# A planned hybrid trunk kernel on one core: paired coupling products, PSUM banks and weight buffers freed later, y split when landed, a masked quarter filled first

## The chip, the cores and the metric

The kernel runs on one core of a Trainium2 chip. The metric is the device time of one execution in microseconds (us). Three runs of the kernel before gave 2273.69, 2272.05 and 2272.64 us; their median is 2272.64.

## The reference

One layer over 2048 positions of width 1024, all in f32. An RMS norm is followed by one input projection, whose columns feed two groups of heads.

```python
proj = einsum('bsd,de->bse', rmsnorm(h, norm_w), w_in)
# group A, 8 groups of 128 columns, blocks of 128 positions
y_a = gelu(u) * (W_masked @ layernorm(gelu(v)) + b) * silu(z)     # W: 128x128, the block (first 64, last 64) is masked
# group B, 8 heads of 128, chunks of 64 positions
q, k, v = silu(causal_conv(qkv));  q, k = l2norm(q) / sqrt(128), l2norm(k)
A = strict_lower((k * beta) @ k.T * L);  T = inverse(A + I)
u = T @ (v * beta);  w = T @ (k * beta * exp(decay));  qk = q @ k.T * L
for each chunk:  v_new = u - w @ S;  o = q_dec @ S + qk @ v_new;  S = S * a + k_dec.T @ v_new
y_b = rmsnorm(o) * norm_w * silu(z)
h = h + concat(y_a, y_b) @ w_out
h = h + sigmoid(rmsnorm(h) @ w_gate) * rmsnorm(p @ w_ple);  out = rmsnorm(h)
```

The state S runs through all chunks of a head in order, and T is the inverse of a unit lower triangular matrix.

## The kernel before

The 2048 positions are worked in two passes of 1024, each of two blocks b of 512. A pass has four units for v of group A (v_unit, lines 498 to 534) and then, for each of eight heads h, three units of 256 columns of w_in: kq_unit (lines 677 to 692), vu_unit (636) and zz_unit (648). A unit projects its 256 columns as four PSUM banks of 128 columns by 512 positions (proj, line 398). Every f32 factor of a large product is split into a high and a low part of type f32r (split, line 211), and each product is made of three matmuls: high by high, high by low, low by high (mm3, line 215). So a bank takes 8 x 3 = 24 matmuls of 512 columns. After the second pass come the output projection (out_stream, 1111), with y read back from DRAM, and the gate (gate_stream, 1254).

Beside the projection, TensorE (PE) has small work for the heads. In front (line 730) k is transposed into the bank pk, from which ACT sums squares and DVE makes kd; the products pkq of two chunks at a time give AT and QK. Two chunks of 64 are handled as one pair of 128. AT goes to DRAM, and inverse (line 838) lays all systems of a head across 128 partitions and solves them by 63 steps on POOL, reading ain in 16 pieces. The two inverses of a pair come back into the diagonal quarters of AT. join (line 887) then couples the two halves of each pair with four products pgt. chain (line 901) runs the state through the eight pairs of a head, and finish (line 974) normalises, transposes into po_t and stores y.

The order of all instructions is written out by a planner that runs when the kernel is built (Flow, lines 31 to 100). It keeps a clock for PE (fl.t) and one for DVE, ACT and POOL, adds a modelled cost for each instruction, and runs its tasks as Python generators: a task yields the time at which it wants to go on, and among those that are due the one with the lowest priority number goes first. The stream of projections is issued between the tasks. On the chip every engine runs its instructions in the order in which they were issued, and semaphores hold them back where data is not ready. All loads and stores go through the queue of SyncE (SP).

Buffers and banks are counted: take (line 68) waits until a place is free, give (line 73) returns it. CAPS (line 105) holds the counts: two PSUM banks each for pj, tr and m, four raw tiles for loaded weights, five split weight pairs w. A give stands right behind the instruction that reads the bank last, so that the place counts as free when that reader is issued. later (line 288) gives a place back at a stated time:

```python
        def later(tag, at):
            yield at
            fl.give(tag)
```

load_w (line 247) loads the four quarters of a unit's weights into raw; split_w (line 256) makes hi on ACT and lo on DVE. The first quarter of the next unit is split in the middle of a unit, the others at k = 1, 3 and 5 of its last bank (rest_w, line 281), when the running unit gives its own pairs back. y_feed (line 1063) loads pieces of y into the raw tiles and splits each as soon as a w place is free; it is started ahead of the last zz_unit, behind refill (line 1026), which loads and splits w_out. zz_unit loads ws, then clears its masked quarter (lines 650 to 652). v_unit keeps ab and the head's first state S0 in tiles of their own.

Of the kernel before, what the change touches and what calls it, by code (L numbers as in the profile page):

```python
# [103 lines left out]
SPARE = 120.0  # L104
CAPS = {"pj": 2, "tr": 2, "m": 2, "kq": 5, "pre": 2, "acc": 3, "uz": 3, "ot": 2, "gn": 2, "R": 2, "raw": 4, "w": 5}
TABLES = {AF.Exp: 1, AF.Sigmoid: 2, AF.Silu: 3, AF.Gelu_apprx_tanh: 4}


def trunk(tc, a, out):
# [78 lines left out]
    with ExitStack() as outer:  # L188
# [58 lines left out]
        def load_w(i):  # L247
            if i < len(units):
                while i and (i - 1, 3) not in W:
                    yield fl.t + 200  # L250
                for kp in range(4):
                    yield from fl.take("raw")
                    raws[i, kp] = wp.tile([P, 2, 256], F32, tag="raw", bufs=4, name="raw")
                    dma(raws[i, kp], a["wu"][units[i], kp])
# [143 lines left out]
        def proj(X, ui, c, b, mid=None):  # L398
            yield pj_free
            fl.used["pj"] = fl.used.get("pj", 0) + 1  # L400
            ps = bank("pj", "pj", [P, 512])
            cc = slice(c * P, c * P + P)
            for k in range(NK):
                if c == 0 and b == 0 and k % 2 == 0:
                    yield lambda: (ui, k // 2) in W
                hi, lo = W[ui, k // 2]
                yield from mm3(ps, hi[:, k % 2, cc], lo[:, k % 2, cc], X[k][0][:, b], X[k][1][:, b],
                               k == 0, k == NK - 1)
                if b and c and k % 2:
                    fl.give("w")  # L410
                if mid and k in mid:
                    mid[k]()
            return ps

        def proj_both(X, ui, c, mid):

            banks = []
            for b in range(2):
                yield pj_free
                fl.used["pj"] = fl.used.get("pj", 0) + 1  # L420
                banks.append(bank("pj", "pj", [P, 512]))
            cc = slice(c * P, c * P + P)
            for k in range(NK):
                hi, lo = W[ui, k // 2]
                for b in range(2):
                    yield from mm3(banks[b], hi[:, k % 2, cc], lo[:, k % 2, cc], X[k][0][:, b], X[k][1][:, b],
                                   k == 0, k == NK - 1)
                if k % 2:
                    fl.give("w")
                mid[k]()  # L430
            return banks
# [66 lines left out]
        def v_unit(X, p, ui, n, stats):  # L498

            fetch(ui + 1)  # L500
            rest = rest_w(ui + 1)
            ab = gt("ab", "ab", [P, 16, 8], 1) if n == 0 else None
            w = 256 if n else 272
# [6 lines left out]
            for group, where in groups:  # L510
# [6 lines left out]
                for k in range(NK):  # L517
                    if p == 0 and n == 0:
                        yield lambda: xready[group[0] // 4] > k
                    yield lambda: len(X) > k and (ui, k // 2) in W  # L520
                    hi, lo = W[ui, k // 2]
                    for t, tag, ps in banks:
                        tk = slice((t % 4) * P, (t % 4) * P + P)
                        yield from mm3(ps[:, :w], X[k][0][:, t // 4, tk], X[k][1][:, t // 4, tk],
                                       hi[:, k % 2, :w], lo[:, k % 2, :w], k == 0, k == NK - 1)
                    if group[-1] == 7:
                        if k % 2:
                            fl.give("w")
                        if k in rest:
                            rest[k]()  # L530
# [15 lines left out]
        def mix(p, g, gz, ws, bs, gns, norms):  # L546
# [10 lines left out]
            for b in range(2):  # L557
# [12 lines left out]
                f = stt(gn, pm, lng[:, g:g + 1], bs[:, None, :].to_broadcast([P, 4, P]), ALU.mult, ALU.add)  # L570
                fl.give("m")
                yf = gn.rearrange("p a b -> p (a b)")
# [75 lines left out]
        def zz_unit(X, p, ui, h, st, norms, mids):  # L648
            fetch(ui + 1)
            ws = gt("ws", "ws", [P, P], 1)  # L650
            dma(ws, a["ws"][h])
            nc.vector.memset(ws[64:128, 0:64], 0.0)
            bs = gt("bs", "bs", [P, P], 1)
            dma(bs, bsd[h] if p else a["bs"][h])
# [46 lines left out]
        def decay(p, h, b, i):  # L701
# [22 lines left out]
            f = act(L, pd, AF.Exp, after=f)  # L724
            fl.give("m")
            yield f + LAZY
# [3 lines left out]
        def front(p, h, b, st):  # L730
# [33 lines left out]
            for u2 in range(2):  # L764
                while len(st["C"][b]) < 2:
# [17 lines left out]
                for j in range(2):  # L783
# [9 lines left out]
                fl.give("m")  # L793
            nc.vector.memset(AT[0:64, :, 64:128], 0.0)
# [8 lines left out]
            fl.spawn(side(b, st, kq, vn, iv, ss, qe), 0, 2)  # L803
            st["B"].append((kq, kd, vn, AT, QK, bn, fb, qe, nb))
            if b == 1:
# [6 lines left out]
        def side(b, st, kq, vn, iv, ss, qe):  # L812
# [5 lines left out]
            f = yield from squares(pq, ss, 4, f)  # L818
            fl.give("tr")
            yield f  # L820
# [11 lines left out]
            yield from fl.room("dve")  # L832
            tt(vn, pv, iv[:, :, None].to_broadcast([P, 4, P]), ALU.mult)
            fl.give("tr")
            fl.give("acc")
            st["R"].append(b)

        def inverse(p, h, st):
# [37 lines left out]
            for b in range(2):  # L876
                for d in range(2):
                    dd = slice(d * 64, d * 64 + 64)
                    dma(st["B"][b][3][dd, :, dd], td[:, b, :, d])
            st["S"] = gt("S0", "S0", [P, P], 1) if p else None  # L880
            if p:
                dma(st["S"], ssc[h])
            fl.spawn(join(0, st), 6500, 0)
            fl.spawn(join(1, st), 7100, 1)
            fl.spawn(chain(p, h, st), 6500, 0)

        def join(b, st):

            M, fb = st["B"][b][3], st["B"][b][6]
            yield from fl.take("tr")  # L890
            pg = bank("tr", "pgt", [P, 4, 64])
            for u in range(4):
                f = mm(pg[:, u], M[:, u], M[:, u, 64:128], True, True)
            yield f
            f = tt(M[0:64, :, 64:128], pg[0:64], fb[0:64, :, None].to_broadcast([64, 4, 64]), ALU.mult)
            fl.give("tr")
            nc.vector.memset(M[64:128, :, 0:64], 0.0)
            yield fl.op("dve", 250) + SPARE
            st["G"].append(b)

        def chain(p, h, st):
# [6 lines left out]
            for b in range(2):  # L908
                kq, kd, vn, M, QK, bn, fb, qe, nb = st["B"][b]
                yield from fl.take("ot")  # L910
# [63 lines left out]
        def finish(p, h, b, st, ot, sso, qe, f):  # L974
# [14 lines left out]
            f = stt(y, pt.rearrange("p a b -> p (a b)"), gdnw, y, ALU.mult, ALU.mult)  # L989
            fl.give("tr")  # L990
            yield f + 200
# [71 lines left out]
        def y_feed():  # L1063
            tiles = {}

            def load(i):
                _, t, e4 = order[i]
                tk = slice((t % 4) * P, (t % 4) * P + P)
                tiles[i] = wp.tile([P, 4, P], F32, tag="raw", bufs=4, name="yraw")
# [26 lines left out]
        def out_piece(WO, key, ps, free):  # L1096
# [3 lines left out]
            for e in range(4):  # L1100
# [6 lines left out]
                if e % 2:  # L1107
                    free.append(1)
            fl.give("w")

# [143 lines left out]
        def gate_stream():  # L1254
            for t in range(NT):
# [14 lines left out]
                for half in range(2):  # L1270
# [3 lines left out]
                    for k in range(NK):  # L1274
# [6 lines left out]
                        if half and k % 4 == 3:  # L1281
                            fl.give("w")
                    if half == 1:
# [3 lines left out]
        def stream():  # L1287
            X = X0
            ui = 0
            for p in range(NPASS):  # L1290
                stats = gt("stats", "stats", [P, 8, 4, 6], 1)
                for n in range(4):
# [137 lines left out]
```

## Time and profile before

| what | value |
|---|---|
| median of three runs | 2272.64 us |
| the profiled execution's own time | 2273.43 us |
| its span, first to last instruction | 2271.7 us |
| mean granted TensorE clock | 0.995 |
| busy: PE / DVE / ACT / POOL | 98% / 59% / 47% / 49% of the span |
| largest share of the chain that ended last | PE 87% |
| DMA | 254.59 MB, 112 GB/s over the span |

The profile shows one execution. "Busy" is the time in which an engine runs at least one instruction. A matmul is recorded from its start to its end, and matmuls overlap, so the distance from one start to the next tells what a matmul costs; the recorded length is longer. A f32 matmul is recorded as two. In a timeline, like instructions that follow one another are merged and counted (x8); the bracket behind a row gives the engine's idle time before it and what ended it.

### The profile page before, as it was taken

How to read it: one execution, taken by the hardware profiler on the slowest of the kernel's cores; microseconds unless marked ns; L12 is line 12 of the kernel's file. 1: busy time of each engine (PE TensorE's matmuls, PEld its weight loads, DVE VectorE, ACT ScalarE, POOL GpSimd, SP SyncE). 2: the span in 40 equal slices, each digit the busy share in tenths (PEclk: the TensorE clock that was granted, in tenths of full speed). 3: DMA queues.
4: the chain of work that ended last, by engine and by line, in shares of the span. 5: the costliest groups of instructions: out<-in, count | busy, mean ns of one | idle time of the engine just before them, and what ended most of it. 6: DMA issues, size and time to landing. Idle time of an engine off the chain costs nothing.

```text
span 2271.7 us, 35525 instructions
## 1 busy us (share of the span) xinstructions
PE 2228.3 (98%) x11888; PEld 1888.4 (83%) x11888; DVE 1335.0 (59%) x2947; ACT 1078.3 (47%) x2541; POOL 1120.3 (49%) x2246
## 2 busy tenths in 40 slices
PE   8999999999999999999999999999899999999998
PEld 8988888888888889988888888888788878878886
DVE  4475675675676664456667567567564243356665
ACT  5554464554554644445546555455433232244443
POOL 1018868687686682058866868768550000001111
PEclk9999999999999999999999999999999999999999
DMA  5733323323323253232332332332453475452221
GB/s 168 250 100 106 101 74 97 97 81 108 95 77 105 72 174 93 81 106 77 94 100 77 94 92 80 108 97 77 137 181 122 145 232 171 141 169 84 84 75 58
DMA packets 269432, 254.59 MB, mean 112 GB/s; under 512 B 67905, under 2 KB 200513, under 8 KB 269249
## 3 DMA queue, kind: packets, MB, share of 16 engines
q1 hardware_dynamic: 269248, 252.32, 36.2%
q8 instruction: 94, 1.54, 0.3%
q14 instruction: 90, 0.73, 0.1%
HBM read 196.68 MB, written 55.57 MB: 111 GB/s over the span
## 4 chain that ended last, share of the span: by engine, by line
PE 87%; DVE 3%; ACT 3%; DMA 3%; POOL 1%; issue 1%; SPq 1%; DVEq 0%; POOLq 0%; ACTq 0%
PE pj L123 41%; PE pso L123 15%; PE pg L123 8%; PE pv L123 7%; PE pc L123 5%; PE po L123 2%; PE pkq L123 2%; PE pe L123 2%; ACT junk L137 1%; PE pm L123 1%; PE pgt L123 1%; PE po_t L129 1%; DMA ws<-in_ws 1%; PE ph L129 1%; PE pq L129 1%
## 5 line engine op out<-in xcount | busy, mean ns | idle before, releaser
L181 POOL TENSOR_TENSOR xtmp<-ain,xs 128x132 f32<-128x132 f32 (+47 forms) x1008 | 460.3, 457 | 269.5 <-DMA ain<-atd 198.7
L181 POOL TENSOR_TENSOR xs<-xs,xtmp 128x132 f32<-128x132 f32 (+47 forms) x1008 | 475.7, 472 | 79.0
L177 POOL TENSOR_TENSOR rstd<-rstd,nhalf 128x1 f32<-128x1 f32 x64 | 45.9, 723 | 576.6 <-DVE rstd L161 295.6
L123 PE MATMUL pj<-xrhi,whi 128*128 128x512 f32 x768 | 312.2, 407 | 0.0
L123 PE MATMUL pj<-xhi,wlo 128*128 128x512 f32 x768 | 310.2, 404 | 0.0
L123 PE MATMUL pj<-xrhi,wlo 128*128 128x512 f32 x768 | 309.9, 404 | 0.0
L123 PE MATMUL pj<-xrlo,whi 128*128 128x512 f32 x768 | 309.9, 403 | 0.0
L123 PE MATMUL pj<-xhi,whi 128*128 128x512 f32 x768 | 309.4, 403 | 0.0
L123 PE MATMUL pj<-xlo,whi 128*128 128x512 f32 x768 | 308.6, 402 | 0.0
L154 DVE SCALAR_TENSOR_TENSOR acc<-pre,cw,acc 128x512 f32<-128x512 f32 x288 | 224.5, 779 | 37.6 <-ACT acc L137 32.9
L150 DVE TENSOR_TENSOR wlo<-raw,whi 128x512 fp32r<-128x512 f32 x224 | 165.7, 742 | 119.0 <-ACT whi L137 116.7
L123 PE MATMUL pso<-wolo,yhi 128*128 128x512 f32 x512 | 204.0, 399 | 0.6 <-DVE wolo L150 0.5
L123 PE MATMUL pso<-wohi,ylo 128*128 128x512 f32 x512 | 203.8, 398 | 0.0
L123 PE MATMUL pso<-wohi,yhi 128*128 128x512 f32 x512 | 202.9, 396 | 0.4 <-ACT zb L137 0.4
L137 ACT ACTIVATE yhi<-yraw 128x512 fp32r<-128x512 f32 x128 | 80.3, 630 | 217.5 <-PE pso L123 203.1
L150 DVE TENSOR_TENSOR ylo<-yraw,yhi 128x512 fp32r<-128x512 f32 x128 | 89.8, 703 | 148.9 <-ACT yhi L137 142.0
L137 ACT ACTIVATE whi<-raw 128x512 fp32r<-128x512 f32 x224 | 139.1, 625 | 62.4 <-PE pj L123 25.8
L123 PEld LDWEIGHTS pj<-xrhi,wlo 128*128 128x128 f32 x768 | 145.4, 189 | 26.2
L123 PEld LDWEIGHTS pj<-xlo,whi 128*128 128x128 f32 x768 | 144.8, 189 | 26.3
L123 PEld LDWEIGHTS pj<-xrhi,whi 128*128 128x128 f32 x768 | 145.5, 189 | 25.4 <-ACT z L137 0.2
L123 PEld LDWEIGHTS pj<-xhi,whi 128*128 128x128 f32 x768 | 145.0, 189 | 25.4
L123 PEld LDWEIGHTS pj<-xrlo,whi 128*128 128x128 f32 x768 | 145.4, 189 | 24.8
(196 smaller groups left out, 4923.8 us busy)
## 6 DMA issues: line engine op xcount, KB each, us to landing
raw<-in_wu SPq DMA_DIRECT2D x224, 256.0 KB
ain<-atd SPq DMA_DIRECT2D x256, 128.0 KB
yraw<-ysc SPq DMA_DIRECT2D x128, 256.0 KB
vsc<-gv SPq DMA_DIRECT2D x64, 128.0 KB
gn<-vsc SPq DMA_DIRECT2D x32, 256.0 KB
ysc<-gn SPq DMA_DIRECT2D x32, 256.0 KB
ysc<-zb SPq DMA_DIRECT2D x32, 256.0 KB
wo<-in_wo SPq DMA_DIRECT2D x32, 256.0 KB
```

The source lines that it names most:

```text
L123: nc.tensor.matmul(o, lhsT, rhs, start=start, stop=stop)
L129: nc.tensor.transpose(o, i, ident)
L137: nc.scalar.activation(o, i, func, **kw)
L150: nc.vector.tensor_tensor(o, x, y, op)
L154: nc.vector.scalar_tensor_tensor(o, x, sc, y, op0, op1)
L177: nc.gpsimd.tensor_tensor(o, x, y, ALU.pow)
L181: nc.gpsimd.tensor_tensor(o, x, y, op)
```

## The change

It has eight parts.

1. The coupling in join: front now writes the scaled quarter to a tile of its own, XC, for all 128 partitions (ex[:, 3] in place of ex[64:128, 3]), and join makes two products for two pairs each, 128 x 128, in place of four with 64 columns. Of each result two quarters are used, one from partitions 0 to 63, one from 64 to 127. fb is copied to the partitions 64 to 127 for this, and the memset of AT's lower left quarter in join goes.
2. The banks of tr and m that were given back when their last reader was issued are given back when the planner expects that reader to have ended, plus 100 ns.
3. The w places are given back 500 ns later.
4. There are three raw tiles and not four.
5. y_feed waits until 5500 ns behind the issue of a piece's load before it takes a w place and splits.
6. In zz_unit the masked quarter of ws is cleared first, and the load comes in two parts that leave it out.
7. The first state of a head in the second pass is loaded by a task of its own, state_in, into the rotating tiles S, once the previous head's chain is planned; chain waits for it.
8. ab and stats live in the tiles of XC.

```diff
-CAPS = {..., "raw": 4, "w": 5}
+CAPS = {..., "raw": 3, "w": 5}
...
                 if b and c and k % 2:
-                    fl.give("w")
+                    fl.spawn(later("w", fl.t + 500))
...
-            ab = gt("ab", "ab", [P, 16, 8], 1) if n == 0 else None
+            ab = gt("XC", "ab", [P, 16, 8], 4) if n == 0 else None
...
             ws = gt("ws", "ws", [P, P], 1)
-            dma(ws, a["ws"][h])
             nc.vector.memset(ws[64:128, 0:64], 0.0)
+            fl.op("dve", 120)
+            dma(ws[0:64], a["ws"][h, 0:64])
+            dma(ws[64:128, 64:128], a["ws"][h, 64:128, 64:128])
...
-            tt(kd, pk, ex[:, 1, cs, None].to_broadcast([P, 4, P]), ALU.mult, after=f)
-            fl.give("tr")
+            fk = tt(kd, pk, ex[:, 1, cs, None].to_broadcast([P, 4, P]), ALU.mult, after=f)
+            fl.spawn(later("tr", max(f1, fk) + 100))
...
             tt(fb, bn, ex[:, 3, cs], ALU.mult)
+            vcopy(fb[64:128], fb[0:64])
...
+            XC = gt("XC", "XC", [P, 4, 64], 4)
...
-                tt(AT[64:128, us, 0:64], pkq[64:128, :, 0, 0:64],
-                   ex[64:128, 3, c:c + 2, None].to_broadcast([64, 2, 64]), ALU.mult)
+                tt(XC[:, us], pkq[:, :, 0, 0:64], ex[:, 3, c:c + 2, None].to_broadcast([P, 2, 64]), ALU.mult)
...
-                fl.give("m")
+                fl.spawn(later("m", f + 100))
...
-            st["S"] = gt("S0", "S0", [P, P], 1) if p else None
-            if p:
-                dma(st["S"], ssc[h])
+            fl.spawn(state_in(p, h, st), 0, 0)
...
+        def state_in(p, h, st):
+            while len(chained) < st["i"]:
+                yield fl.t + 300
+            if p:
+                st["S"] = gt("S", "S0", [P, P], 2)
+                dma(st["S"], ssc[h])
+            else:
+                st["S"] = None
...
-            pg = bank("tr", "pgt", [P, 4, 64])
-            for u in range(4):
-                f = mm(pg[:, u], M[:, u], M[:, u, 64:128], True, True)
-            yield f
-            f = tt(M[0:64, :, 64:128], pg[0:64], fb[0:64, :, None].to_broadcast([64, 4, 64]), ALU.mult)
+            pg = bank("tr", "pgt", [P, 2, 2, 64])
+            for i in range(2):
+                f = mm(pg[:, i], XC[:, 2 * i:2 * i + 2].rearrange("p u j -> p (u j)"),
+                       M[:, 2 * i:2 * i + 2, 64:128], True, True)
+            yield f
+            for j in range(2):
+                half = slice(j * 64, j * 64 + 64)
+                f = tt(M[0:64, j:4:2, 64:128], pg[half, :, j], fb[half, j:4:2, None].to_broadcast([64, 2, 64]),
+                       ALU.mult)
             fl.give("tr")
-            nc.vector.memset(M[64:128, :, 0:64], 0.0)
-            yield fl.op("dve", 250) + SPARE
+            yield f + SPARE
...
-            while len(chained) < st["i"] or len(st["R"]) < 2:
+            while len(chained) < st["i"] or len(st["R"]) < 2 or "S" not in st:
...
             def load(i):
+                at[i] = fl.t + 5500
...
+                yield at[i]
                 yield from fl.take("w")
```

The same later gives stand in proj_both, v_unit, out_piece and gate_stream (w), in mix and decay (m), and in side and finish (tr).

## Rows read from the trace of the kernel before

**Rows 1.** The page's first part: busy us, share of the span, instructions.
```profile
PE 2228.3 (98%) x11888; PEld 1888.4 (83%) x11888; DVE 1335.0 (59%) x2947; ACT 1078.3 (47%) x2541; POOL 1120.3 (49%) x2246
```

**Rows 2.** PE's waits: what waited for what, us in total, times, longest.
```profile
PE po_t L129 <- DVE kd L150: 7.2, 5, 1.6
PE pc L123 <- ACT r L137: 6.8, 2, 6.4
...
PE pkq L123 <- DVE kqlo L150: 2.8, 9, 0.5
...
PE pc L123 <- DVE w L159: 1.8, 3, 1.1
...
PE pc L123 <- DVE r L154: 0.9, 2, 0.7
```

**Rows 3.** Timeline of PE at a mix and at a join: start, us, what.
```profile
193.70 1.05 PE L123 MATMUL pm<-ws,gn 128*128 128x128 f32 x8
194.51 0.47 PE L123 MATMUL pj<-xhi,wlo 128*128 128x512 f32 x1
...
1606.18 1.00 PE L123 MATMUL pgt<-AT 128*128 128x64 f32 x8
1607.02 0.44 PE L123 MATMUL pc<-S,kq 128*128 128x128 f32 x2
```

**Rows 4.** Groups of PE instructions: count, busy us, mean ns, idle before.
```profile
L123 PE MATMUL pgt<-AT 128*128 128x64 f32 x256 | 31.5, 270 | 0.5 <-DVE AT L150 0.5
```

**Rows 5.** Groups of DVE instructions around the join.
```profile
L150 DVE TENSOR_TENSOR AT<-pkq,ex 64x128 f32<-64x128 f32 x64 | 18.8, 294 | 2.2
L150 DVE TENSOR_TENSOR AT<-pgt,fb 64x256 f32<-64x256 f32 x32 | 13.3, 414 | 15.0 <-PE pgt L123 14.7
...
L897 DVE MEMSET AT<- 64x256 f32 x32 | 8.7, 272 | 3.0
```

**Rows 6.** Timeline from 503 us: DVE's kd and PE's transposes.
```profile
503.17 0.69 DVE L150 TENSOR_TENSOR kd<-pk,ex 128x512 f32<-128x512 f32 x1 [0.63 <-ACT junk L137]
...
503.91 0.66 PE L129 MATMUL po_t<-ident,ot 128*128 128x128 f32 x4 [1.42 <-DVE kd L150]
```

**Rows 7.** Timeline from 1609 us: the first y loads, their split, PE.
```profile
1609.29 2.81 SPq L1070 DMA_DIRECT2D yraw<-ysc  x4
...
1615.32 0.63 ACT L137 ACTIVATE yhi<-yraw 128x512 fp32r<-128x512 f32 x1 [9.69 <-DMA yraw<-ysc]
...
1616.64 0.80 PE L123 MATMUL pc<-r,AT 128*128 128x128 f32 x2 [6.44 <-ACT r L137]
```

**Rows 8.** Stretches: us; busy (count) of PE, PEld, DVE, ACT, POOL; PEclk; DMA.
```profile
125.00:827.00 702.00, 693.28 (x3642) 581.78 (x3641) 463.30 (x1073) 370.11 (x916) 501.69 (x1015) 1.00 0.33 98
...
1600.00:1605.00 5.00, 5.00 (x25) 4.11 (x24) 1.47 (x4) 4.25 (x12) 0.00 (x0) 1.00 0.54 136
...
1617.00:1622.00 5.00, 5.00 (x16) 4.13 (x16) 0.99 (x3) 0.79 (x4) 2.65 (x8) 0.50 0.81 222
```

**Rows 9.** Tile pc from 505 to 575 us: ns min/median/max, first and last start.
```profile
L123 PE MATMUL pc<-w,kd x16: 270/274/323, 527.3 to 572.6; 128*128 128x128 f32 x16
```

**Rows 10.** DVE's waits: us in total, times, longest.
```profile
DVE ws L652 <- DMA ws<-in_ws: 33.7, 14, 6.3
```

**Rows 11.** Timeline from 1341 us: the memset of ws and PE behind it.
```profile
1341.60 0.11 DVE L652 MEMSET ws<- 64x64 f32 x1 [1.90 <-DMA ws<-in_ws]
...
1342.24 0.46 PE L123 MATMUL pc<-w,kd 128*128 128x128 f32 x2 [1.12 <-DVE w L159]
```

**Rows 12.** Waits of SyncE's queue: us in total, times, longest.
```profile
SPq L254 <- DVE wlo L150: 187.3, 88, 11.1
```

**Rows 13.** Timeline of the start: the last constant, the first unit's last split.
```profile
17.86 0.33 SPq L198 DMA_DIRECT2D alog<-in_alog  x1
...
21.60 0.62 ACT L137 ACTIVATE whi<-raw 128x512 fp32r<-128x512 f32 x1
```

More of the change, by code (lines that the diff above doesn't have):

```diff
@@ L104 @@
 SPARE = 120.0
-CAPS = {"pj": 2, "tr": 2, "m": 2, "kq": 5, "pre": 2, "acc": 3, "uz": 3, "ot": 2, "gn": 2, "R": 2, "raw": 4, "w": 5}
+CAPS = {"pj": 2, "tr": 2, "m": 2, "kq": 5, "pre": 2, "acc": 3, "uz": 3, "ot": 2, "gn": 2, "R": 2, "raw": 3, "w": 5}
 TABLES = {AF.Exp: 1, AF.Sigmoid: 2, AF.Silu: 3, AF.Gelu_apprx_tanh: 4}
@@ L252, in load_w @@
                     yield from fl.take("raw")
-                    raws[i, kp] = wp.tile([P, 2, 256], F32, tag="raw", bufs=4, name="raw")
+                    raws[i, kp] = wp.tile([P, 2, 256], F32, tag="raw", bufs=3, name="raw")
                     dma(raws[i, kp], a["wu"][units[i], kp])
@@ L428, in proj_both @@
                 if k % 2:
-                    fl.give("w")
+                    fl.spawn(later("w", fl.t + 500))
                 mid[k]()
@@ L527, in v_unit @@
                         if k % 2:
-                            fl.give("w")
+                            fl.spawn(later("w", fl.t + 500))
                         if k in rest:
@@ L724, in decay @@
             f = act(L, pd, AF.Exp, after=f)
-            fl.give("m")
+            fl.spawn(later("m", f + 100))
             yield f + LAZY
@@ L788, in front @@
                 c = h * 8 + b * 4 + u2 * 2
-                tt(AT[64:128, us, 0:64], pkq[64:128, :, 0, 0:64],
-                   ex[64:128, 3, c:c + 2, None].to_broadcast([64, 2, 64]), ALU.mult)
+                tt(XC[:, us], pkq[:, :, 0, 0:64], ex[:, 3, c:c + 2, None].to_broadcast([P, 2, 64]), ALU.mult)
                 yield from fl.room("dve")
                 f = tt(QK[:, u2 * 2:u2 * 2 + 2], pkq[:, :, 1], L[:, u2 * 2:u2 * 2 + 2], ALU.mult)
-                fl.give("m")
+                fl.spawn(later("m", f + 100))
             nc.vector.memset(AT[0:64, :, 64:128], 0.0)
@@ L803, in front @@
             fl.spawn(side(b, st, kq, vn, iv, ss, qe), 0, 2)
-            st["B"].append((kq, kd, vn, AT, QK, bn, fb, qe, nb))
+            st["B"].append((kq, kd, vn, AT, QK, bn, fb, qe, nb, XC))
             if b == 1:
@@ L818, in side @@
             f = yield from squares(pq, ss, 4, f)
-            fl.give("tr")
+            fl.spawn(later("tr", f + 100))
             yield f
@@ L832, in side @@
             yield from fl.room("dve")
-            tt(vn, pv, iv[:, :, None].to_broadcast([P, 4, P]), ALU.mult)
-            fl.give("tr")
+            f = tt(vn, pv, iv[:, :, None].to_broadcast([P, 4, P]), ALU.mult)
+            fl.spawn(later("tr", f + 100))
             fl.give("acc")
@@ L885, in inverse @@
             fl.spawn(chain(p, h, st), 6500, 0)
+        def state_in(p, h, st):
[6 more added lines that the diff above has]
+                st["S"] = None
         def join(b, st):
-            M, fb = st["B"][b][3], st["B"][b][6]
+            M, fb, XC = st["B"][b][3], st["B"][b][6], st["B"][b][9]
             yield from fl.take("tr")
-            pg = bank("tr", "pgt", [P, 4, 64])
-            for u in range(4):
-                f = mm(pg[:, u], M[:, u], M[:, u, 64:128], True, True)
+            pg = bank("tr", "pgt", [P, 2, 2, 64])
+            for i in range(2):
+                f = mm(pg[:, i], XC[:, 2 * i:2 * i + 2].rearrange("p u j -> p (u j)"),
+                       M[:, 2 * i:2 * i + 2, 64:128], True, True)
             yield f
-            f = tt(M[0:64, :, 64:128], pg[0:64], fb[0:64, :, None].to_broadcast([64, 4, 64]), ALU.mult)
+            for j in range(2):
+                half = slice(j * 64, j * 64 + 64)
+                f = tt(M[0:64, j:4:2, 64:128], pg[half, :, j], fb[half, j:4:2, None].to_broadcast([64, 2, 64]),
+                       ALU.mult)
             fl.give("tr")
-            nc.vector.memset(M[64:128, :, 0:64], 0.0)
-            yield fl.op("dve", 250) + SPARE
+            yield f + SPARE
             st["G"].append(b)
@@ L908, in chain @@
             for b in range(2):
-                kq, kd, vn, M, QK, bn, fb, qe, nb = st["B"][b]
+                kq, kd, vn, M, QK, bn, fb, qe, nb, XC = st["B"][b]
                 yield from fl.take("ot")
@@ L989, in finish @@
             f = stt(y, pt.rearrange("p a b -> p (a b)"), gdnw, y, ALU.mult, ALU.mult)
-            fl.give("tr")
+            fl.spawn(later("tr", f + 100))
             yield f + 200
@@ L1063, in y_feed @@
         def y_feed():
-            tiles = {}
+            tiles, at = {}, {}
             def load(i):
+                at[i] = fl.t + 5500
                 _, t, e4 = order[i]
                 tk = slice((t % 4) * P, (t % 4) * P + P)
-                tiles[i] = wp.tile([P, 4, P], F32, tag="raw", bufs=4, name="yraw")
+                tiles[i] = wp.tile([P, 4, P], F32, tag="raw", bufs=3, name="yraw")
                 dma(tiles[i], ysc[t // 4][4 * e4:4 * e4 + 4, :, tk].rearrange("e p t -> p e t"))
@@ L1108, in out_piece @@
                     free.append(1)
-            fl.give("w")
+            fl.spawn(later("w", fl.t + 500))
         def out_stream():
@@ L1281, in gate_stream @@
                         if half and k % 4 == 3:
-                            fl.give("w")
+                            fl.spawn(later("w", fl.t + 500))
                     if half == 1:
@@ L1290, in stream @@
             for p in range(NPASS):
-                stats = gt("stats", "stats", [P, 8, 4, 6], 1)
+                stats = gt("XC", "stats", [P, 8, 4, 6], 4)
                 for n in range(4):
```

## The prediction

> **What bounds the kernel now.** I read the busy times first: TensorE (PE) is busy for 2228.3 of 2271.7 us, the other engines for 47 to 59% [rows 1]. So the time is the sum of PE's own work plus 43.4 us in which it stands still. Only two things can shorten it: fewer PE instructions, or fewer of those halts. Work on DVE, ACT, POOL or a queue counts only where PE waits for it. The second view is therefore PE's waits [rows 2]. The longest are transposes po_t that wait for DVE's kd (7.2 us in 5 times) and the chain's pc that waits for ACT's r (6.8 us, of which one halt is 6.4). The third view is the timeline around each of these.
>
> **The paired products.** A join issues four products with 64 columns each; the trace records them as eight matmuls, and 0.84 us pass from their first start, 1606.18, to the next instruction at 1607.02 [rows 3]. The mix issues four products with 128 columns, also eight records, and takes 0.81 us from 193.70 to 194.51 [rows 3]. So twice the columns cost nothing more: a product of this kind has a price per instruction, 0.20 us. After the change a join has two products with 128 columns: 2 x 0.81/4 = 0.41 us in place of 0.84, 0.43 us less. There are 32 joins (256 records of eight, [rows 4]): 13.9 us. Bounds: half of 0.84 gives 13.4, half of the group's busy time of 31.5 us [rows 4] gives 15.8. I take 13.9, the nearest like for like.
>
> The Trainium skill (page "TensorE: Matmul & The Clock Gate", section "Back-to-back issue gap") puts the gap between matmuls at the columns streamed, about 60 cycles up to 64 columns and 134 for 128. By that, two of 128 cost what four of 64 cost and this term would be nil. The rows above disagree with it.
>
> Around the join, DVE loses one product of 0.414 us and one memset of 0.272 [rows 5] and gains two of 64x128; such a one (AT<-pkq,ex) takes 0.294. So 0.69 becomes 0.59. The XC product spans 128 partitions but the same 128 elements in each, so I leave it at 0.294. The copy of fb is new: under the 0.272 of the larger memset, 32 times, so at most 9 us over a DVE that is idle for 41% of the span [rows 1]. All this is free as long as PE has projection matmuls to run meanwhile; if that cover were gone, the copies' 0.27 us would stand in each of 32 fronts.
>
> **Banks given back when read.** The planner gave the bank of pk free once kd was issued. At 503.91 PE came to the transposes po_t, placed in that bank, and stood 1.42 us until DVE's kd, started at 503.17, had ended [rows 6]. The five such halts are the 7.2 us of [rows 2]. Now the bank counts as free 100 ns after the later of the squares and kd, so the planner puts projection matmuls there. It estimates that end; where its estimates are off, PE waits about 0.3 us (pkq for kqlo, 2.8 us in 9 times [rows 2]). I keep 5 x 0.3 = 1.5 us as lost: gain 5.7. Bounds: 0, if po_t then meets another late release, and 7.2. The other late releases (m, and tr after pq, pvt, po_t) answer to no PE wait among the long ones: nothing gained; what they delay is covered by projections, and without that cover each would cost its 0.1 us and the planner's 0.15 us step.
>
> **y split when landed.** At the last head, SyncE issues the y loads from 1609.29 on. ACT's first yhi has been put in its queue before the chain's copy r, starts only at 1615.32 when y lands, and PE, waiting for r, goes on at 1616.64 after 6.44 us [rows 7]. It comes back at half clock: from 1617 to 1622 the granted clock is 0.50, which is the 1.2 GHz level, and 16 PE instructions run in 5 us, against 25 at 1.00 just before the halt [rows 8]. Half of 5 us is lost, 2.5. Together 8.9 us. After the change the split is put 5.5 us behind the load by the planner's clock. That clock doesn't see SyncE's issues in front (six wo loads end just before 1609.29), so the load is planned near 1606 and the split comes to ACT near 1611.5. It then still holds ACT for up to 1615.3 - 1611.5 = 3.8 us. Chain steps are 45.3/7 = 6.5 us apart (x16 records, two a step, 527.3 to 572.6 [rows 9]), so PE may miss that hole or meet it: 0 to 3.8 us. I take the middle, 1.9, without the half clock: gain 7.0, bounds 0 and 8.9. The 1.9 us are the first thing late in its place. With three raw buffers y is read three deep and not four; behind that stand up to four split pieces in the w buffers, twelve matmuls each, which at 0.20 us [rows 8] are 9.6 us of cover, longer than the 6.0 us from 1609.29 to 1615.32. No cost; without the cover, the rest of a load per piece.
>
> **The masked quarter ahead of its load.** DVE's memset of ws waits for its DMA 33.7 us in all [rows 10]. At one of them the load lets the memset go at 1341.60, and PE, waiting for the w queued behind it, has stood 1.12 us when it goes on [rows 11]. PE's three waits for w make 1.8 us [rows 2]; most of DVE's 33.7 is idle time that costs nothing. I take 1.8; bounds 0 and 2.7, if PE's 0.9 us of waits for DVE's r [rows 2] come from ws too. SyncE issues 16 loads more, past which bs, gn and raw move; no one waits for these at that point, though y is pushed by one issue. The three parts of ws don't overlap, so the loads need not wait for the memset; if they do, SyncE stands until DVE comes to it, with bs, gn and ain behind, a few us that POOL's slack takes.
>
> **Buffers.** The w buffers come back 0.5 us later. The last quarter is split from k=5 of a unit's last bank and needed 27 matmuls later, 5.4 us at 0.20 [rows 8]: covered. Three raw buffers put the fourth load of each unit behind the first split; SyncE then waits for DVE's wlo once more a unit, with ain and gn loads behind it. It does so already 88 times, 2.1 us each [rows 12]: three units a head, 6.4 us, taken by POOL's slack. In the first unit the fourth load falls behind eight x loads and six constants, to about 18 us, where the last constant is issued at 17.86 [rows 13]; its split starts at 21.60. Were it there at once this would cost nothing; with the 6.0 us that y took under a full DMA load it would be 2.3 us late. I take 1.1, the middle. The state load (S) leaves at the same moment as before when the previous chain is over, 6.5 us of plan ahead of its reader: nothing; without that cover, a load's few us in each of eight heads.
>
> **Sum.** 13.9 + 5.7 + 7.0 + 1.8 - 1.1 = 27.3 us. The profiled execution took 2273.43 us, 0.8 above the median of 2272.64. 2272.6 - 27.3 = 2245.3, so 2245.
>
> **Rivals.**
> First, *the waits only move*: the planner's order shifts in every head, and halts of the po_t kind come up at other places as often as they leave. For it: where a halt falls is an accident of phase, and every later step of the plan shifts. Against it: the release is now tied to the reader. Then only pairing and a part of y stay, about 15 us: 2258.
> Second, *products cost by column*: the pairing brings nothing and the rest holds, 2245 + 14 = 2259. Against it stand both rows of [rows 3].
> Third, *the new order falls better*: all upper bounds, 15.8 + 7.2 + 8.9 + 2.7 = 34.6 us, 2238.
> Fourth, slower: *SyncE holds up the inverse*. The extra wait for wlo in mid-unit delays ain, POOL's inverse ends later and with it the chain, until the next fronts wait for it and PE runs dry. A chain takes about 45 of the 88 us of a head (702 us for eight [rows 8]). The fronts two heads on need its first half, so I estimate 20 us of slack. It decides from there: each wait would have to be 7 us and not 2.1 (the longest is 11.1 [rows 12]). At 11.1 the slip is 33 us, 13 over; were only 3 us of that to reach PE in 14 heads, 42 us: 2245 + 42 = 2287.
>
> **How the numbers follow.** Forecast 0.62; waits only move 0.17; by column 0.05; better order 0.08; slower 0.05; the remaining 0.03 is a gain eaten down to nothing. About 0.2%, 4.5 us, is what a measurement of this kernel tells from no change. Faster by more: 0.91; within: 0.04; slower: 0.05. The range takes in the forecast with its bounds, the better order and the moved waits: 2234 to 2262.
>
> **What would show it.** Pairing: pgt has 128 records of 128 columns and not 256 of 64, and about 0.42 us a join. Banks: no po_t <- kd wait above 0.5 us. y: the halt near 1616 is under 4 us and the clock stays at 1.00 behind it. ws: no DVE wait for its DMA. It would be wrong if PE's idle time rose beyond 43 us, or if new waits recur at one point of every head.

## The result and the profile after

The changed kernel takes 2257.89 us (median of 4 runs, 2255.71 to 2258.90) against 2272.90 for the kernel before beside it. The ratio is 0.9933, with an interval of 0.9916 to 0.9950: 15.0 us faster. The forecast was 27 us faster; the result lies in the range and on the right side, but it is almost the number of the first rival, *the waits only move* (2258). The profiled executions show nearly the same difference: 2258.90 against 2273.43 us, 14.5. The profiled execution is the longest of the four, at a mean granted clock of 0.995; the shortest had 0.997.

The page's first part after the change, which answers to [rows 1]:

```profile
span 2257.2 us, 35348 instructions
...
PE 2216.2 (98%) x11760; PEld 1875.3 (83%) x11760; DVE 1330.1 (59%) x2979; ACT 1080.1 (48%) x2539; POOL 1120.6 (50%) x2246
```

PE has 128 instructions fewer and is busy 12.1 us less. But the span less the busy time, 41.0 us, is almost what it was (43.4). By the forecast the halts should have lost some 11 us (the 13.4 beside pairing, less the 2.5 of half clock in y's term). So the work went as forecast and the halts did not.

PE's waits after the change (us in total, times, longest), to be read against [rows 2]:

```profile
PE pc L123 <- DVE r L154: 6.8, 3, 3.7
PE pkq L123 <- DVE kqlo L150: 4.8, 10, 1.1
PE pv L123 <- DVE ab L169: 3.8, 2, 2.6
...
PE po_t L129 <- DVE kd L150: 1.5, 3, 0.8
PE pc L123 <- DVE AT L150: 1.3, 1, 1.3
...
PE pgt L123 <- DMA AT<-td: 1.3, 1, 1.3
...
PE pc L123 <- DVE S L154: 0.9, 1, 0.9
```

The waits that the change aimed at have shrunk: po_t for kd from 7.2 to 1.5 us, the chain's wait for w from 1.8 to none. Others stand in their place: AT, td and S had no such row before, kqlo grew by 2.0, and the three waits for r (0.9 before) hold two that have to be found: 3.7 us, and 2.0.

**The joins.** The group of pgt, then PE's timeline at two joins:

```profile
L123 PE MATMUL pgt<-AT,XC 128*128 128x128 f32 x128 | 19.0, 277 | 2.3 <-DMA AT<-td 1.3 <-PE pc L123 0.5 <-issue 0.5
```

```profile
1074.99 0.71 PE L123 MATMUL pgt<-AT,XC 128*128 128x128 f32 x4 [1.32 <-DMA AT<-td]
1075.56 0.49 PE L123 MATMUL pc<-S,kq 128*128 128x128 f32 x2
1075.88 0.61 PE L123 MATMUL pgt<-AT,XC 128*128 128x128 f32 x4
1076.25 0.47 PE L123 MATMUL pj<-xrhi,whi 128*128 128x512 f32 x1
```

The second join takes 0.37 us from its first start, 1075.88, to the next instruction, against 0.84 before [rows 3]. Summed from each start to the next, the 256 records of before [rows 4] took 26.97 us and the 128 of now take 13.13: 13.8 less, the forecast's term to a tenth.

**The last head.** Its timeline after the change, beside [rows 7]:

```profile
1602.85 2.82 SPq L663 DMA_DIRECT2D gn<-vsc  x2
...
1606.53 0.63 ACT L137 ACTIVATE yhi<-yraw 128x512 fp32r<-128x512 f32 x1 [6.15 <-DMA yraw<-ysc]
1607.19 0.70 DVE L150 TENSOR_TENSOR ylo<-yraw,yhi 128x512 fp32r<-128x512 f32 x1 [4.64 <-ACT yhi L137]
...
1608.01 0.34 DVE L154 SCALAR_TENSOR_TENSOR r<-pc,ne,vn 128x128 f32<-128x128 f32 x1
...
1608.40 0.80 PE L123 MATMUL pc<-r,AT 128*128 128x128 f32 x2 [3.72 <-DVE r L154]
```

ACT's yhi still stands in its queue before y has landed, DVE's ylo behind yhi, and r behind ylo. PE halts for 3.72 us, not 6.44.

**The start of the second pass.** The same chain of waits is new here, with x in y's place. This is a timeline of the changed kernel while the v units run and the last chain of the first pass ends:

```profile
818.36 0.49 PE L123 MATMUL pc<-r,AT 128*128 128x128 f32 x2 [1.00 <-DVE r L154]
...
825.36 0.63 ACT L137 ACTIVATE xrhi<-xr 128x512 fp32r<-128x512 f32 x1 [4.09 <-DMA xr<-xsc]
826.02 0.72 DVE L150 TENSOR_TENSOR xrlo<-xr,xrhi 128x512 fp32r<-128x512 f32 x1 [2.46 <-ACT xrhi L137]
...
827.50 0.34 DVE L154 SCALAR_TENSOR_TENSOR r<-pc,ne,vn 128x128 f32<-128x128 f32 x1
...
827.90 0.49 PE L123 MATMUL pc<-r,AT 128*128 128x128 f32 x2 [2.03 <-DVE r L154]
...
840.89 0.57 PE L123 MATMUL pv<-whi,xrhi 128*128 128x272 f32 x1 [2.62 <-DVE ab L169]
```

In the kernel before, PE's timeline from 815 to 850 us shows these waits and no others:

```profile
821.40 0.46 PE L123 MATMUL pc<-w,kd 128*128 128x128 f32 x2 [0.35 <-DVE w L159]
...
825.61 0.49 PE L123 MATMUL pc<-r,AT 128*128 128x128 f32 x2 [0.18 <-DVE r L154]
...
844.85 0.36 PE L123 MATMUL pv<-whi,xrhi 128*128 128x272 f32 x1 [2.36 <-DVE ab L169]
```

So the halt for ab was there before. The halts of 1.00 and 2.03 us for r ahead of it are new, and in this trace the clock falls at the halt for ab. These are stretches of the changed kernel (us; busy us and count of PE, PEld, DVE, ACT, POOL; granted clock; DMA share; GB/s), first at the last head, then at the start of the second pass:

```profile
1604.50:1608.40 3.90, 0.19 (x1) 0.00 (x0) 1.16 (x3) 1.17 (x4) 3.27 (x9) 0.98 1.11 306
1608.40:1612.00 3.60, 3.60 (x11) 3.07 (x12) 0.69 (x1) 2.56 (x6) 1.66 (x5) 0.55 0.73 206
...
838.50:840.89 2.39, 0.00 (x0) 0.03 (x1) 1.13 (x4) 2.36 (x5) 2.00 (x6) 0.86 0.12 21
840.89:844.00 3.11, 3.11 (x14) 3.09 (x15) 1.26 (x6) 0.19 (x1) 2.56 (x8) 0.50 0.70 229
844.00:847.50 3.50, 3.50 (x19) 3.50 (x19) 1.59 (x4) 0.38 (x1) 3.09 (x8) 0.56 0.48 162
847.50:851.00 3.50, 3.50 (x31) 3.50 (x30) 0.00 (x0) 0.40 (x2) 2.74 (x10) 1.00 0.00 1
```

0.50 is the 1.2 GHz level. As an estimate, the time lost to it is the missing share of the clock times the stretch: 0.45 x 3.6 = 1.6 us at the last head, 0.50 x 3.11 + 0.44 x 3.50 = 3.1 us at the start of the pass.

The ledger, from these rows and those of before:

| what | before, us | after, us | difference |
|---|---|---|---|
| products of the joins | 26.97 | 13.13 | -13.8 |
| po_t for kd | 7.2 | 1.5 | -5.7 |
| the halt at the last head | 6.44 | 3.72 | -2.7 |
| the chain for w | 1.8 | 0 | -1.8 |
| every other wait of PE | | | +7.8 |
| half clock behind the last head's halt | 2.75 | 1.6 | -1.15 |
| half clock at the start of pass 2 | 0 | 3.1 | +3.1 |

The 2.75 us of before are 5 us at 0.50 [rows 8] and the next 5, to 1627, at 0.95. The +7.8 is what remains of the 2.4 us by which PE's idle time fell, once the three rows above it (-10.2) are taken out. The start of pass 2 is 3.3 of it (1.00 + 0.20 + 2.03 + 2.62 against 0.18 + 2.36; the 0.20 is a wait for ACT's r at 819.26, and the 0.35 for w of before stands in w's own row), kqlo 2.0, AT, td and S 3.5; small waits that went take 1.0 back. The sum is -14.3 of the measured -14.5. Since the +7.8 is a remainder, only the other half of the sum is a test: the joins and the two half clocks, which are part of PE's busy time, make -11.9, and that time fell by 12.1.

### The profile page after: what moved, and what is told of

The parts are those of the page before. It is cut to its first block, busy times and chain, and to the rows that moved or that the text cites. A ratio compares the mean times of both kernels' runs of the same rounds, so it can differ in the third digit from the quotient of the medians.

```text
span 2257.2 us, 35348 instructions
## 1 busy us (share of the span) xinstructions
PE 2216.2 (98%) x11760; PEld 1875.3 (83%) x11760; DVE 1330.1 (59%) x2979; ACT 1080.1 (48%) x2539; POOL 1120.6 (50%) x2246
## 4 chain that ended last, share of the span: by engine, by line
PE 86%; POOL 3%; DVE 3%; DMA 3%; ACT 3%; issue 1%; SPq 1%; POOLq 0%; DVEq 0%; ACTq 0%
PE pj L123 39%; PE pso L123 15%; PE pv L123 8%; PE pg L123 8%; PE pc L123 5%; PE po L123 2%; PE pkq L123 2%; PE pe L123 2%; POOL xs L181 1%; POOL xtmp L181 1%; ACT junk L137 1%; PE pm L123 1%; DMA wo<-in_wo 1%; PE po_t L129 1%; PE pgt L123 1%
## 5 line engine op out<-in xcount | busy, mean ns | idle before, releaser
L181 POOL TENSOR_TENSOR xtmp<-ain,xs 128x132 f32<-128x132 f32 (+47 forms) x1008 | 450.1, 447 | 254.8 <-DMA ain<-atd 184.7
L181 POOL TENSOR_TENSOR xs<-xs,xtmp 128x132 f32<-128x132 f32 (+47 forms) x1008 | 483.4, 480 | 79.0
L123 PEld LDWEIGHTS pj<-xhi,wlo 128*128 128x128 f32 x768 | 144.9, 189 | 25.2
```

The source lines that it names most:

```text
L123: nc.tensor.matmul(o, lhsT, rhs, start=start, stop=stop)
L181: nc.gpsimd.tensor_tensor(o, x, y, op)
```

## The experiments

The ledger says where the time went, not why. Times are compared as ratios to the kernel before on the same chip; 0.001 is 2.3 us. The changed kernel itself stands at 0.9933.

**Pairing undone.** The changed kernel with the old join.

```diff
-                f = mm(pg[:, i], XC[:, 2 * i:2 * i + 2].rearrange("p u j -> p (u j)"),
-                       M[:, 2 * i:2 * i + 2, 64:128], True, True)
+            for u in range(4):
+                f = mm(pg[:, u], M[:, u], M[:, u, 64:128], True, True)
```

> The changed kernel with the old join: four products of 64 columns, the old quarter of AT and the memset; everything else stays. If a product costs per instruction (0.20 us each), this gives back 13.9 us: about 2272, pgt again 256 records. If products cost by column, nothing: about 2258.

Measured: 2261.32 us, ratio 0.9943 (0.9932 to 0.9955). That is only 2.3 us above the changed kernel, less than the intervals can tell from nothing, where 13.9 were expected. Yet PE has its 11.7 us of work back, as the page shows, and the wait for r is nearly gone:

```profile
PE 2227.9 (98%) x11888; PEld 1888.1 (83%) x11888; DVE 1334.6 (59%) x2947; ACT 1082.3 (48%) x2541; POOL 1125.2 (50%) x2246
...
PE pkq L123 <- DVE kqlo L150: 4.7, 11, 1.0
...
PE pc L123 <- DVE r L154: 0.8, 1, 0.8
```

The stretches that hold the start of pass 2 (818 to 936 us) and the last head (1544 to 1635 us) both have a granted clock of 1.00 here, against 0.97 and 0.98 in the changed kernel. At these two places PE's halts of over 0.9 us are one of 1.09 here and 1.00, 2.03, 2.62 and 3.72 in the changed kernel. So with the longer joins the plan misses most of the two load-dependent halts and with the shorter ones it meets them: pairing's work is gone, and much of its gain is spent there.

**Three raw tiles alone.** One explanation was that SyncE, which has three raw tiles now and waits more for wlo (343.8 us against 187.3, [rows 12]), issues everything behind that later. The kernel before with "raw": 3 in place of 4:

> The kernel before with three raw tiles in place of four, nothing else. Theory: the third tile makes SyncE stand for DVE's wlo (187 us before, 344 after the change), loads behind it come late, and that ate part of the gain: 4 to 8 us slower than before, 2277 to 2281, SyncE's wait for wlo over 300 us. Rival, the waits only move by accident of phase: within 2 us of 2273.

Measured: 2273.34 us, ratio 0.9992 (0.9983 to 1.0001), no loss. The longest of SyncE's waits in that run:

```profile
SPq L254 <- DVE wlo L150: 395.1, 135, 12.5
```

Twice the waiting on that queue cost nothing in the kernel before. The explanation loses its ground.

**Pairing without the other mends.** The kernel before with the parts 1, 4, 7 and 8; banks, w places, y and ws as before.

> The paired join with the tiles it needs (XC, ab and stats in it, three raw tiles, S by its own task), but banks, w places, y and ws as before. Theory: -13.9 for pairing, +4 to +8 for the raw tiles: 2263 to 2267, with the po_t halts (7 us) and the y halt (9 us) still there. Rival (moved waits): the same as the whole change, 2258, within 2.

Measured: 2279.92 us (2274.93 to 2287.94 in 10 runs), ratio 1.0030 (1.0018 to 1.0043): slower than before, with PE's busy time down to 2216.7 us. Its waits of PE:

```profile
PE pc L123 <- DVE r L154: 11.4, 3, 7.9
PE pc L123 <- DVE AT L150: 6.2, 4, 1.8
...
PE po_t L129 <- DVE kd L150: 4.5, 3, 1.6
...
PE pc L123 <- DVE w L159: 3.0, 4, 1.8
```

The expectation missed, and so did its rival. The work saved is there, but the chain's waits for r (from DVE and ACT) and for AT, 7.7 us in all in the kernel before [rows 2], are 19.9 (11.4, 6.2 and 2.3 for ACT's r). The halt at the last head is 7.9 us, where it was 6.44; two halts for r, 1.35 and 1.26, are new at the start of pass 2; and all four waits for AT stand behind the memset of ws, which waits 44.2 us in all for its load. These rows are of the shortest of the ten executions. The times go with the mean granted clock, 0.996 at 2274.93 us and 0.991 to 0.993 in the four above 2282; what lowers it more in one execution than in another isn't settled.

**Raw tiles given back later in the plan.** A last trial of the raw tiles: in the changed kernel, raw counts as free only when the planner expects wlo to be done.

```diff
-                fl.give("raw")
+                fl.spawn(later("raw", f + 100))
```

> The changed kernel, but a raw tile counts as free 100 ns after the planned end of its wlo and not when wlo is issued, as the change does it for banks. Theory: SyncE's wait for wlo falls well under 344 us, loads of ain, td and xr come earlier, and the new halts (pgt behind AT's load, the chain's r behind xr) go: 2248 to 2253. Rival: SyncE's waits fall but PE's halts don't care: 2258, within 3.

Measured: 2259.96 us, ratio 0.9933 (0.9922 to 0.9945). SyncE's waits for wlo fell to 282.3 us from 343.8, the time didn't, and the halt for AT's load didn't go (1.8 us; 1.3 in the changed kernel). With the run of three raw tiles alone this leaves nothing that speaks for that queue.

**One part undone at a time.** The banks of tr and m given back at issue again; y split without its wait; the whole ws loaded ahead of the memset:

```diff
-                fl.spawn(later("m", f + 100))
+                fl.give("m")
...
-                yield at[i]
...
+            dma(ws, a["ws"][h])
             nc.vector.memset(ws[64:128, 0:64], 0.0)
-            fl.op("dve", 120)
-            dma(ws[0:64], a["ws"][h, 0:64])
-            dma(ws[64:128, 64:128], a["ws"][h, 64:128, 64:128])
```

> The changed kernel with the banks of tr and m given back at the issue of their last reader, as before. If the later release is worth its term, the po_t behind kd halts come back: 5.7 us slower than the changed kernel, about 2264. If halts only move: within 2 us of 2258.

> The changed kernel without the wait for y's landing: the split is issued at once. Forecast term: the halt near the last head grows from 3.7 to 6.4 us and the half clock with it: 3.5 to 7 us slower, 2261 to 2265. Rival: y's place doesn't matter, within 2 us of 2258.

> The changed kernel with the whole ws loaded first and its quarter cleared behind the load. DVE's wait for ws comes back (about 34 us); by its term PE loses 1.8 us: about 2260. Rival: DVE's idle time is free, 2258 within 1.

Measured: banks 2263.99 us, 0.9956 (0.9943 to 0.9970), +5.2 us; y 2262.35 us, 0.9945 (0.9933 to 0.9958), +2.7; ws 2264.43 us, 0.9958 (0.9945 to 0.9970), +5.7. Each interval overlaps that of the changed kernel, so the single differences are good to some 4 us. The old ws cost more than its 1.8 us and more than its rival allowed. What the rows show is firmer. Without the banks' part po_t waits 4.5 us for kd again, 3.0 more; the rest of that difference isn't in po_t. Without y's wait the halt at the last head is 7.2 us. And without the third the memset's wait shows in PE's path, at a place where the kernel before had no such wait. The timeline of the run with the old ws:

```profile
706.42 0.11 DVE L652 MEMSET ws<- 64x64 f32 x1 [4.53 <-DMA ws<-in_ws]
706.54 0.30 DVE L169 COPY r<-vn 128x128 f32<-128x128 f32 x1
706.77 1.20 DVE L150 TENSOR_TENSOR AT<-pgt,fb 64x128 f32<-64x128 f32 x4
...
707.10 0.49 PE L123 MATMUL pc<-r,AT 128*128 128x128 f32 x2 [2.43 <-DVE AT L150]
```

DVE stands 4.53 us at the memset, with the join's AT queued behind it, and PE with it for 2.43. All waits for AT are 6.7 us in 4 times there. The run with pairing and the old ws had the same row (6.2 in 4 times). So beside the paired joins PE's waits behind the old memset are longer than the 1.8 us of before: in the 6.7 the wait for AT of the changed kernel is 1.3.

**The y loads first.** In the changed kernel the six loads of w_out stand in SyncE's queue ahead of the first y, issued at 1597.02 and for 3.88 us, so y's load begins later than the planner counts. y_feed is started ahead of refill, and refill 200 ns later:

```diff
-                            fl.spawn(refill(gp, free, [[a["wo"][0, e2, :, e] for e in range(2)] for e2 in range(8)],
-                                            WO0, "wo"), 0, 1)
                             fl.spawn(y_feed(), 0, 1)
+                            fl.spawn(refill(gp, free, [[a["wo"][0, e2, :, e] for e in range(2)] for e2 in range(8)],
+                                            WO0, "wo"), 200, 1)
```

> The changed kernel with y's loads issued ahead of w_out's (the two tasks started in the other order, the second 200 ns later). SyncE then issues y 3 us earlier, and its planned 5.5 us hold: ACT doesn't stand at yhi, the 3.7 us halt of PE and its half clock behind go: 2253, 5 us faster. If the landing is set by the bytes in flight and not by SyncE's order, the halt stays: 2258.

Measured: 2251.78 us, ratio 0.9900 (0.9886 to 0.9913), 7.5 us under the changed kernel. The timeline around the split:

```profile
1601.12 0.64 ACT L137 ACTIVATE yhi<-yraw 128x512 fp32r<-128x512 f32 x1 [1.81 <-DMA yraw<-ysc]
1601.79 0.69 DVE L150 TENSOR_TENSOR ylo<-yraw,yhi 128x512 fp32r<-128x512 f32 x1 [0.30 <-ACT yhi L137]
```

ACT's wait is 1.81 us, not 6.15, and no halt of PE follows; from 1602 to 1616 the granted clock stays at 1.00. The halt and its half clock are 3.72 + 1.6 = 5.3 us in the ledger; the other 2.2 are within the intervals.

**All staged loads split when landed.** The run above, and refill's pieces of x, w_out and w_gate also wait until 5500 ns behind their load.

```diff
-            staged[j] = tiles
+            staged[j] = (fl.t + 5500, tiles)
...
+            at, tiles = staged.pop(j)
+            yield at
```

> The changed kernel with y's loads ahead of w_out's, and the splits of the staged pieces (x of the second pass, w_out, w_gate) also put 5.5 us behind their loads. Theory: the halts at the boundary of the passes, where the chain's r stands behind xrhi and xrhi behind the load of xr (1.0 and 2.0 us after the change), go: 2247 to 2250, PE's halts in the second pass's v units back from 9.7 to about 6 us. Rival: they come up elsewhere, 2252.

Measured: 2254.02 us, ratio 0.9911 (0.9897 to 0.9924): no gain, a miss. At the start of pass 2 it does what it should. From the last matmul into pj of the first pass to the first of the second, which is the time of the v units and the small work between them, the trace has 122.4 us in the changed kernel (118.0 before) and 119.2 here. The stretch from 817 to 939 us, first in the changed kernel, then in this one:

```profile
817.00:939.00 122.00, 116.11 (x940) 114.66 (x939) 57.25 (x151) 55.20 (x128) 36.49 (x78) 0.97 0.33 104
```

```profile
817.00:939.00 122.00, 118.28 (x955) 116.08 (x954) 59.75 (x163) 55.69 (x129) 39.82 (x80) 0.99 0.36 110
```

PE stands 2.2 us less in it, and the granted clock is nearly whole. But the wait also delays pieces of w_out and w_gate that have long landed: PE now waits 1.2 us for wglo and 1.1 for wolo in the last stages, where no such wait for wglo stood before.

**The same without pairing.** The old join in the kernel above.

> The same with the old join of four products. If undoing the pairing cost so little (2 us) only because that order happened to miss the two places where a split waits for a load, then with both places mended in both kernels the work comes through: 13.9 us slower than the run above, 2261 to 2264. If the halts depend on phase whatever is mended, the two are 2 to 6 us apart.

Measured: 2265.97 us, ratio 0.9962 (0.9948 to 0.9975), on the same chip as the run with pairing: 12.0 us slower (11.6 by the ratios, good to some 4). The first experiment had shown 2.3 for the same edit. With the splits put behind the loads in both kernels, the 13.9 us of PE's work come through almost whole.

**More releases tied to their reader, later joins.** v_post's banks too are given back at the planned end of their reader, and join and chain start 1500 ns later.

```diff
-            fl.give(tag)
+            fl.spawn(later(tag, f + 100))
...
-            fl.spawn(join(0, st), 6500, 0)
-            fl.spawn(join(1, st), 7100, 1)
-            fl.spawn(chain(p, h, st), 6500, 0)
+            fl.spawn(join(0, st), 8000, 0)
+            fl.spawn(join(1, st), 8600, 1)
+            fl.spawn(chain(p, h, st), 8000, 0)
```

> As the run before the last, and the v units' banks are also given back when ab and gv are planned to be read, and join and chain start 1.5 us later behind the loads of AT. Theory: PE's waits for ab (4 us) and for AT's load (1.8 us) go: 2243 to 2246. Rival, a halt that goes at one place comes at another: within 2 us of the run with the landings alone.

Measured: 2250.03 us, ratio 0.9892 (0.9878 to 0.9907), 4 us less than the run with all staged loads. That is short of the 2243 to 2246 expected, and more than the rival allowed. The wait for td is gone and that for ab is 1.9 us, but halts of 3.5 us for r and 3.8 for xlo are new: in part a halt that goes at one place did come at another. Which of the two edits did what wasn't tried apart.

**Only x waits for its load.** The same, with the wait in refill for the pieces of x alone.

```diff
-                yield at
+                if name == "xr":
+                    yield at
```

> As the run before, but only the pieces of x wait for their landing; w_out and w_gate are split as soon as a place is free, as in the changed kernel. Theory: in the output projection a staged piece has long landed, and the added wait only made it late (PE's halts there 4.6 to 5.4 us, 1.7 without): 3 us come back, 2244 to 2248. Rival: these halts were phase too, 2250 within 2.

Measured: 2243.14 us (2241.76 to 2244.03), ratio 0.9868 (0.9851 to 0.9884). It beats both kernels, by 30 us and 15 us. The stretch from 817 to 939 us and the longest waits:

```profile
817.00:939.00 122.00, 120.53 (x972) 118.00 (x971) 61.21 (x167) 58.55 (x134) 35.58 (x69) 1.00 0.36 111
...
PE pc L123 <- DVE r L154: 4.3, 2, 3.8
PE pkq L123 <- DVE kqlo L150: 3.9, 9, 1.1
PE ptx L129 <- DVE xlo L154: 3.8, 1, 3.8
```

PE stands 1.5 us in this stretch and not 5.9, at full clock throughout, and the v units take 115.9 us where they took 122.4. In the output projection the waits for wohi and wolo fell from 2.7 us to 0.7; that is less than half of the 5.5 us by which the ratio fell against the run before, and the two intervals overlap. Two halts of 3.8 us are left, and the one for r has the same chain of waits at a third place, the split of a unit's weights:

```profile
789.95 0.63 ACT L137 ACTIVATE whi<-raw 128x512 fp32r<-128x512 f32 x1 [6.28 <-DMA raw<-in_wu]
790.61 0.87 DVE L150 TENSOR_TENSOR wlo<-raw,whi 128x512 fp32r<-128x512 f32 x1 [4.60 <-ACT whi L137]
```

DVE's r starts behind them, at 791.66, and PE goes on at 792.06.

## Why the prediction was right, and where not

**Pairing: right, to a tenth.** 13.9 us were forecast and 13.8 measured. A product of these costs the same with 64 and with 128 columns, 0.21 us each in the sums above (26.97/128 and 13.13/64); *products cost by column* is refuted. The trace shows 0.37 us for two of 128 against 0.84 for four of 64. The table that the prediction took from the Trainium skill (page "TensorE: Matmul & The Clock Gate", section "Back-to-back issue gap"), with about twice the cycles for 128 columns, is given there for a matmul by itself; of a stream of weight loads and matmuls the same section says that both set the spacing. The second rule, not the first, is in keeping with the 0.21 us; the measurement decides.

**Banks: right, the remainder by luck.** 7.2 to 1.5 us. The term kept 1.5 as five misses of 0.3 us; the trace has three of 0.5 on average. Undoing it costs 5.2 us, of which 3.0 show in po_t. The bar of 0.5 us for the longest such wait was too strict: one of 0.8 remains.

**y: right mechanism, a mis-sized term.** That the planner's clock doesn't see SyncE's issues, and that the split so stands early in ACT's queue, was the stated reason; starting y's loads first removes the halt. But the step "I take the middle, 1.9, without the half clock" failed twice over: the halt is 3.72 us, at the upper bound of 3.8, and the clock fell behind it, 1.6 us. The term of 7.0 measured 2.7 + 1.15 = 3.9 in place.

**ws: right in place, too small.** 1.8 us left PE's waits, and DVE has no wait for ws any more, as forecast. Beside the paired joins it seems to be worth more (+5.7 when undone, good to some 4): there the join's DVE products stand behind the memset. The forecast priced each part against the kernel before; the parts change one another's price.

**Buffers and the start: no cost.** The 1.1 us charged to the first unit weren't found (PE's waits in the first 60 us are 8.1 before and 8.0 after), and three raw tiles alone cost nothing, with twice SyncE's waits of before. That POOL's slack is what takes these waits, the reason given, wasn't shown.

**The step that failed** is the sum itself: "a gain eaten down to nothing" got 0.03 and every other halt was left as it was. The 27.3 us less 3.1 for y, less 7.8 of other waits, less 3.1 of half clock at the start of pass 2, plus the 1.1 not lost, are 14.4, the ledger's sum to a tenth. The range held because it took in the moved waits; the forecast's own sum was 12 us too large. The forecast did name the mechanism, in the rival *the waits only move*, with 0.17: where a halt falls is an accident of phase. What it lacked is where the phase matters. The plan takes an x piece as there when a tile is free, and counts a y piece's 5.5 us without the issues in front of it; on the chip ACT stands at the head of its queue until the load lands (6.15 and 4.09 us), DVE behind ACT, and the chain's r behind both. A change in PE's time shifts the chain's steps against these landings. Undoing pairing moves most of them off (first experiment), pairing alone moves them on, beside the memset (third), and making the splits wait for the landing at the start of pass 2, and y's loads go first, lets the gain through (12.0 us in the tenth). Part of the half clock is chance besides: the run with raw given back later has the same halts at the start of pass 2 and none of its 3.1 us. One slip in the chances changes nothing: the rivals as listed make 0.92 for faster, not 0.91.

That the 5.5 us of kqlo, AT, td and S come from the same shift of phase is argued, not shown; only td's went with one experiment, the later joins.

## What to carry to other kernels

A shorter bound engine pays only if the halts don't come back elsewhere: before pricing a saving, look for the places where an in-order queue waits at its head for a load that the plan doesn't time, and ask what a shift of a few us would put behind it. Mend these first, by order of the loads or by a wait in the plan, but only for pieces that are really fresh from memory. Judge one part with such halts mended in both kernels; the pairing looked like 2 us, like a loss of 7 (with the tiles it needs), and like 12, by what stood beside it.

## What the runs showed of the hardware

The clock fell to its 1.2 GHz level after halts shorter than the 6.44 us one of before, but not after each of them. In the changed kernel PE stood 3.72 us and then ran at 0.55 for 3.6 us; at the start of pass 2 it stood 2.62 us, 13 us behind a halt of 2.03, and then ran at 0.50 and 0.56 for 6.6 us. In the kernel before, the same wait for ab, 2.36 us, left the clock at 1.00. The halt ahead of it isn't what decides. In the run with raw given back later PE stood 2.04 and 2.63 us at these two places, as far apart, and the clock stayed at 1.00; in the kernel before with three raw tiles it stood 2.35 us for ab with no halt of more than 0.31 in the 25 us ahead, and the clock fell. The stretches behind the halt for ab, first of the one, then of the other:

```profile
842.20:845.50 3.30, 3.15 (x24) 2.97 (x25) 2.33 (x7) 0.61 (x2) 2.75 (x8) 1.00 0.60 202
```

```profile
844.68:848.20 3.52, 3.52 (x16) 3.49 (x17) 1.74 (x7) 0.84 (x4) 2.95 (x8) 0.52 0.66 218
```

So a halt of 2 to 3 us can bring a loss of 1.6 to 3.1 us behind it or none, by the estimate above, and one trace can't tell which a change will get. What decides it stays open.

A queue of SyncE can stand 395 us of a 2274 us span on one kind of wait, twice what it stood, at no cost in time (ratio 0.9992, at most 1.0001).
